# Gate and up projections by Strassen's seven products, SBUF as two arenas, branch and feed-forward tiles through HBM

## The chip, the core and the metric

The kernel runs on one core of a Trainium2 chip. The metric is the time of one execution on the device, in microseconds (us), from the first to the last instruction of the core. The engines are PE (TensorE: matmuls, with PEld for its weight loads), DVE (VectorE), ACT (ScalarE), POOL (GpSimd) and SP (SyncE, which here only issues loads). Each engine works through its own queue of instructions in order; a DMA is issued by one of these queues and ends later on its own.

## The reference, cut to what matters

One decoder block: 512 tokens, width 2048, two branches (latent attention, and a chunked spatial gate), a gated merge, an output projection, and a dense SwiGLU feed-forward of width 5632, all in float32.

```
a = rms_norm(h, g_mix);   z = a @ w_in                   # latents, u, v, gate logits
y_attn = mla(...) @ w_o_attn;   y_sgu = sgu(uv, ...) @ w_o_sgu
merged = sigmoid(g0) * y_attn + sigmoid(g1) * y_sgu
h = h + merged @ w_out
f = rms_norm(h, norm_ffn_g)
h = h + (silu(f @ w_gate_ffn) * (f @ w_up_ffn)) @ w_down_ffn   # [512,2048]x[2048,5632], twice
return rms_norm(h, norm_final_g)
```

## The kernel before

**Products in three passes.** Every float32 operand is split into a high part (an ACT cast to fp32r, line 94 for weights, 81 and 84 for other tiles) and a low part (a DVE subtraction, lines 95, 82, 85). A product is then three matmuls (`mm3`, lines 99 to 101): low by high, high by high, high by low.

**Weights.** `chunk` takes 512 KB of weights at a time: a load on the SP queue (line 93) into one of four `raw` buffers, the cast on ACT into one of three `whi`, the subtraction on DVE into one of three `wlo`. A load waits for the subtraction that read the buffer four chunks earlier. `gemm_fm` uses a chunk of 512 rows by 256 columns for 24 matmuls of 128x512 (feature-major: weights stationary, all 512 tokens moving); `gemm_tm` does the same token-major.

**Stages, in order.** Input statistics and latents, the shared rotary key, v and u of the spatial gate, its mixing (`L328`), transposes of the latents (`L341`), attention over eight pairs of heads, the attention branch, the gates and the merge, `w_out` with the residual, the feed-forward, the final norm. All tiles between the stages stay in SBUF, in one pool of 75 tiles of 512 columns.

**The feed-forward.** `norm_in` transposes the residual h between the four column blocks of `w_out` and splits it with the gain; the division by the root mean square is a factor per token and is put on the results instead (`rfb`, lines 582 and 584). `hidden(mp)` makes 256 columns of the hidden layer: gate and up together in four banks, 16 tiles of 128 rows deep, that is 2 x 16 x 2 x 3 = 192 matmuls of 128x512; 22 such steps make 4224. Then Silu (line 583), the product (585) and its split. After 8, 8, 8, 6, 6 and 8 rows of hidden tiles `down` uses them, so hidden and down alternate.

The engines' queues follow the order in which a scheduler puts the program's instructions; the rows of that order stand below where they matter.

Of the kernel before, what the change touches and what calls it, by code (L numbers as in the profile page):

```python
# [16 lines left out]
P = 128  # L17
# [7 lines left out]
G = 8  # L25
# [16 lines left out]
BIG, WR, WS = 75, 4, 3  # L42
FMAX = float(np.finfo(np.float32).max)


@with_exitstack
def tile_block(ctx: ExitStack, tc, a):
# [3 lines left out]
    big = ctx.enter_context(tc.tile_pool(name="big", bufs=BIG))  # L51
    wraw = ctx.enter_context(tc.tile_pool(name="wraw", bufs=WR))
    wsp = ctx.enter_context(tc.tile_pool(name="wsp", bufs=WS))
# [3 lines left out]
    def T(dt=F32):  # L57
        return big.tile([P, 512], dt, tag="t", name="t")
# [4 lines left out]
    def small(n, tag):  # L63
        return sml.tile([P, n], F32, tag="s%d" % n, name=tag)

# [8 lines left out]
    ones = con[:, C_ONE:C_ONE + P]  # L74

    def split(src, gain=None, n=512):
        hi, lo = T(F32R), T(F32R)
        if n < 512:
            hi, lo, src = hi[:, :n], lo[:, :n], src[:, :n]
        if gain is None:  # L80
            nc.scalar.copy(hi, src)  # L81
            nc.vector.tensor_tensor(out=lo, in0=src, in1=hi.bitcast(F32), op=ALU.subtract)  # L82
        else:
            nc.scalar.activation(hi, src, AF.Copy, scale=gain)
            nc.vector.scalar_tensor_tensor(
                out=lo, in0=src, scalar=gain, in1=hi.bitcast(F32), op0=ALU.mult, op1=ALU.subtract)
        return hi, lo

    def chunk(src, n=1024):
        raw = wraw.tile([P, 1024], F32, tag="raw", name="raw")  # L90
        hi = wsp.tile([P, 1024], F32R, tag="whi", name="whi")
        lo = wsp.tile([P, 1024], F32R, tag="wlo", name="wlo")
# [3 lines left out]
        return hi[:, :n], lo[:, :n]  # L96
# [6 lines left out]
    def gemm_fm(banks, w, kq, xs, first, last):  # L103
        """banks[m] += w[k-quad, 256 columns]^T @ xs (feature-major)."""
        hi, lo = chunk(w)
        hi = hi.rearrange("p (k m) -> p k m", k=4)
        lo = lo.rearrange("p (k m) -> p k m", k=4)
        for m, ps in enumerate(banks):
            ms = slice(m * P, (m + 1) * P)
            for k in range(4):  # L110
                xh, xl = xs[kq * 4 + k]
                mm3(ps, hi[:, k, ms], lo[:, k, ms], xh, xl, first and k == 0, last and k == 3)

    def gemm_tm(banks, w, kp, xs, first, last):
# [24 lines left out]
    def sumsq(parts, n, tag):  # L139
        """Sum of squares along the free axis of each list of tiles: [P, n]."""  # L140
        k = len(parts[0])
        acc = small(n * k, tag + "a")
        for i, tiles in enumerate(parts):
            for j, t in enumerate(tiles):
                junk = T()
# [7 lines left out]
    def row_bcast(r, tag):  # L153
        """[P, NB] per-token columns -> the same values along the free axis on each partition."""
        ps = PS()
        for tb in range(NB):
            dg = T()[:, :P]
            nc.vector.tensor_scalar(out=dg, in0=ident, scalar1=r[:, tb:tb + 1], scalar2=None, op0=ALU.mult)
            nc.tensor.matmul(ps[:, tb * P:(tb + 1) * P], ones, dg, start=True, stop=True)  # L159
        out = T()  # L160
# [4 lines left out]
    def load_x(xs, k):  # L165
        """Tiles 2k and 2k + 1 of the gained x, feature-major."""
        raw = wraw.tile([P, 1024], F32, tag="raw", name="raw")
        nc.sync.dma_start(raw, a["xT"][k])
        for j in range(2):
            v = V_MIX + k * 2 + j  # L170
            xs.append(split(raw[:, j * 512:(j + 1) * 512], vec[:, v:v + 1]))

# [3 lines left out]
    def x_stats(tb):  # L176
        for c in range(4):
            t, junk = T(), T()
            nc.sync.dma_start(t, a["x"][tb * P:(tb + 1) * P, c * 512:(c + 1) * 512])
            nc.scalar.activation(junk, t, AF.Square, accum_out=xacc[:, tb * 4 + c:tb * 4 + c + 1])  # L180

# [6 lines left out]
    lat = []  # L188
    lacc = cst.tile([P, 2 * NB], F32, name="lacc")
    def lat_out(g, banks):  # L190
        row = []
        for tb, ps in enumerate(banks):
            z, junk = T(), T()
# [22 lines left out]
    posi = big.tile([P, 512], I32, tag="t", name="posi")  # L216
# [11 lines left out]
    sinT = cst.tile([P, 512], F32, name="sinT")  # L228
    cosT = cst.tile([P, 512], F32, name="cosT")
# [3 lines left out]
    nc.scalar.activation(cosT, ang, AF.Sin)  # L233

    def rope(src):
        """The rotated [2 x 64 rope features, tokens]."""
        rot, out = T(), T()
# [4 lines left out]
        nc.vector.tensor_tensor(out=out, in0=out, in1=rot, op=ALU.add)  # L242
        return out

# [1 line left out]
    raw = wraw.tile([P, 1024], F32, tag="raw", name="raw")  # L246
    nc.sync.dma_start(raw, a["w_kpe"])
    kps = PS()
    for half in range(2):
        wk = wsp.tile([P, 1024], F32R, tag=("whi", "wlo")[half], name="wk").rearrange("p (k o m) -> p k o m", k=8, o=2)  # L250
# [7 lines left out]
    rxb = row_bcast(rx, "rxb")  # L258
    kpe = T()
    for own, other in ((slice(0, 64), slice(64, 128)), (slice(64, 128), slice(0, 64))):  # L260
        nc.scalar.copy(kpe[own], kps[other])
        nc.vector.tensor_tensor(out=kpe[own], in0=kps[own], in1=kpe[own], op=ALU.add)
    nc.vector.tensor_tensor(out=kpe, in0=kpe, in1=rxb, op=ALU.mult)
# [6 lines left out]
    vv = [[None, None] for _ in range(NB)]  # L270
    for g in range(2):
        banks = [PS() for _ in range(NB)]
        for kp in range(8):
            gemm_tm(banks, a["w_v"][g, kp], kp, aT, kp == 0, kp == 7)
        for tb, ps in enumerate(banks):
            t = T()
            nc.scalar.activation(t, ps, AF.Gelu_apprx_tanh, scale=rx[:, tb:tb + 1])
            vv[tb][g] = t
    rv = rsqrt(sumsq(vv, NB, "sv"), SGUW, NB, "rv")
    for tb in range(NB):  # L280
        for g in range(2):
            nc.vector.tensor_scalar(out=vv[tb][g], in0=vv[tb][g], scalar1=rv[:, tb:tb + 1], scalar2=None,
                                    op0=ALU.mult)

    kpe = rope(kpe)
    kph = cst.tile([P, 512], F32R, name="kph")
    kpl = cst.tile([P, 512], F32R, name="kpl")
    nc.scalar.copy(kph, kpe)
    nc.vector.tensor_tensor(out=kpl, in0=kpe, in1=kph.bitcast(F32), op=ALU.subtract)

    ut = []
    for mp in range(4):
        banks = [PS(), PS()]
        for kq in range(4):
            gemm_fm(banks, a["w_u"][mp, kq], kq, aT, kq == 0, kq == 3)
        for ps in banks:
            t = T()
            nc.vector.tensor_tensor(out=t, in0=ps, in1=rxb, op=ALU.mult)
            nc.scalar.activation(t, t, AF.Gelu_apprx_tanh)
            ut.append(t)  # L300

    wsT = []
    bsb = []
    for half in range(2):
        wt = wraw.tile([P, 1024], F32, tag="raw", name="raw")[:, :512]
        nc.gpsimd.dma_start(wt.rearrange("t (g s) -> t g s", g=4),
                            a["w_sgu"][half * 4:half * 4 + 4].rearrange("g t s -> t g s"))
        wm = wraw.tile([P, 1024], F32, tag="raw", name="raw")[:, :512]
        nc.gpsimd.affine_select(out=wm, in_=wt, pattern=[[0, 4], [-1, P]], compare_op=ALU.is_ge, fill=0.0,
                                base=0, channel_multiplier=1)  # L310
        ps = PS()
        for g in range(4):
            nc.tensor.transpose(out=ps[:, g * P:(g + 1) * P], in_=wm[:, g * P:(g + 1) * P], identity=ident)
        t = T()
        nc.vector.tensor_copy(t, ps)
        wsT.append(t)
        bt = T()
        nc.gpsimd.dma_start(bt, a["b_sgu"][half * 512:half * 512 + 512].partition_broadcast(P))
        bsb.append(bt)

# [1 line left out]
    latT = []  # L322
    for g in range(2):
        rows = []
        for k in range(4):
# [5 lines left out]
            rows.append(split(ps, vec[:, v:v + 1]))  # L331
        latT.append(rows)
    qnT, kvT = latT

# [1 line left out]
    sgT = []  # L336
    for g in range(G):
# [5 lines left out]
        t = T()  # L343
# [5 lines left out]
        nc.vector.tensor_tensor(out=t, in0=t, in1=ut[g], op=ALU.mult)  # L349
        sgT.append(t)  # L350
# [378 lines left out]
```

## Time and profile before

| | |
|---|---|
| time, median of 3 runs | 2789.36 us (2789.19 to 2790.16) |
| span of the profiled execution | 2788.1 us (the page gives no other time for it) |
| PE busy | 2769.5 us, 99% of the span |
| DVE, ACT busy | 1125.1 us (40%), 843.1 us (30%) |
| DMA | 280.07 MB, mean 100 GB/s |
| mean granted TensorE clock | 0.999 |

A row of a group names line, engine, operation, output<-inputs and shape, then how many there are, the busy time, the mean of one, and the idle time before them with what ended it. A row of the timeline has a start, a duration, the instruction, and in brackets the idle time before it with what ended that.

### The profile page before, as it was taken

Reading aid. Unit: us, or ns where it says so; the run is one execution under the profiler, and the core shown is the slowest. Engines: PE = TensorE matmul, PEld = TensorE weight load, DVE = VectorE, ACT = ScalarE, POOL = GpSimd, SP = SyncE. Lnnn points to the kernel's source line nnn. Section 1 sums busy time; section 2 is a strip of 40 time slices with the busy share of each in tenths; the row PEclk is TensorE's granted clock in tenths of the full one; section 3 lists DMA queues with packets and bytes.
Section 4 is the critical chain, followed back from the end, with each engine's and each line's share of the span. In section 5 each row is a group of like instructions: output and inputs, shape, how many; then the busy total and the mean of one; then the engine's idle time right before and its main releaser. Section 6 shows DMA issues by size and latency. Waiting matters only on the chain.

```text
span 2788.1 us, 30320 instructions
## 1 busy us (share of the span) xinstructions
PE 2769.5 (99%) x12712; PEld 2312.9 (83%) x12712; DVE 1125.1 (40%) x1470; ACT 843.1 (30%) x1195; POOL 15.4 (1%) x31
## 2 busy tenths in 40 slices
PE   8999999999999999999999999999999999999998
PEld 7888988888888888888888888888888888888887
DVE  3433867742433333532433333333333333343345
ACT  5332565621322222332322122212221222222223
POOL 0000000000000000100000000000000000000000
PEclk9999999999999999999999999999999999999999
DMA  7323211222423322432223323323222322223232
GB/s 249 101 91 96 79 53 54 70 90 97 154 97 98 98 98 93 153 102 91 91 98 98 99 92 98 98 98 99 94 96 98 98 99 96 94 98 98 99 121 91
DMA packets 79752, 280.07 MB, mean 100 GB/s; under 512 B 9152, under 2 KB 9152, under 8 KB 79616
## 3 DMA queue, kind: packets, MB, share of 16 engines
q1 hardware_dynamic: 76176, 268.99, 29.4%
q0 software_dynamic: 2000, 6.56, 0.7%
q10 hardware_dynamic: 1440, 2.60, 0.3%
q8 instruction: 99, 1.62, 0.2%
q14 instruction: 37, 0.30, 0.0%
HBM read 273.92 MB, written 4.19 MB: 100 GB/s over the span
## 4 chain that ended last, share of the span: by engine, by line
PE 99%; DVE 0%; DMA 0%; ACT 0%; issue 0%; SPq 0%
PE b L99 32%; PE b L101 32%; PE b L100 32%; PE b L446 1%; PE b L425 0%; PE b L426 0%; PE b L546 0%; PE b L341 0%; DMA raw<-in_w_lat 0%; PE b L328 0%; ACT whi L94 0%; DVE wlo L95 0%; PE b L159 0%; DVE t L266 0%; DVE t L82 0%
## 5 line engine op out<-in xcount | busy, mean ns | idle before, releaser
L95 DVE TENSOR_TENSOR wlo<-raw,whi 128x1024 fp32r<-128x1024 f32 (+1 forms) x480 | 583.3, 1216 | 1416.0 <-ACT whi L94 1415.7
L99 PE MATMUL b<-t,wlo 128*128 128x512 f32 x2592 | 1008.8, 389 | 0.0
L101 PE MATMUL b<-t,whi 128*128 128x512 f32 x2592 | 1008.5, 389 | 0.0
L100 PE MATMUL b<-t,whi 128*128 128x512 f32 x2592 | 1008.5, 389 | 0.0
L94 ACT CAST whi<-raw 128x1024 fp32r<-128x1024 f32 (+1 forms) x480 | 501.6, 1046 | 1588.7 <-PE b L101 977.2
L99 PEld LDWEIGHTS b<-t,wlo 128*128 128x128 f32 x2592 | 486.6, 188 | 101.5 <-DVE wlo L95 0.2
L101 PEld LDWEIGHTS b<-t,whi 128*128 128x128 f32 x2592 | 486.6, 188 | 100.9
L100 PEld LDWEIGHTS b<-t,whi 128*128 128x128 f32 x2592 | 486.6, 188 | 100.7
L99 PE MATMUL b<-whi,t 128*128 128x512 f32 (+1 forms) x1280 | 486.3, 380 | 7.9 <-ACT whi L94 7.9
L101 PE MATMUL b<-wlo,t 128*128 128x512 f32 (+1 forms) x1280 | 485.5, 379 | 0.0
L100 PE MATMUL b<-whi,t 128*128 128x512 f32 (+1 forms) x1280 | 485.3, 379 | 0.0
L99 PEld LDWEIGHTS b<-whi,t 128*128 128x128 f32 x1280 | 241.4, 189 | 52.7 <-ACT whi L94 7.9
L101 PEld LDWEIGHTS b<-wlo,t 128*128 128x128 f32 x1280 | 241.3, 188 | 45.8 <-DVE wlo L95 0.8
L100 PEld LDWEIGHTS b<-whi,t 128*128 128x128 f32 x1280 | 241.4, 189 | 45.1
L596 DVE TENSOR_TENSOR t<-b,t 128x512 f32<-128x512 f32 x96 | 66.1, 689 | 32.4 <-PE b L101 31.9
L81 ACT CAST t<-t 128x512 fp32r<-128x512 f32 x84 | 49.3, 623 | 98.4 <-DVE t L585 96.4
L82 DVE TENSOR_TENSOR t<-t 128x512 fp32r<-128x512 f32 x84 | 55.7, 689 | 32.9 <-ACT t L81 32.9
L99 PE MATMUL b<-t 128*128 128x512 f32 (+2 forms) x192 | 66.3, 346 | 1.2 <-DVE t L82 1.2
L100 PE MATMUL b<-t 128*128 128x512 f32 (+2 forms) x192 | 66.3, 345 | 0.0
L101 PE MATMUL b<-t 128*128 128x512 f32 (+2 forms) x192 | 66.2, 345 | 0.0
L82 DVE TENSOR_TENSOR t<-b,t 128x512 fp32r<-128x512 f32 (+1 forms) x96 | 58.2, 662 | 15.6 <-ACT t L81 15.3
L81 ACT CAST t<-b 128x512 fp32r<-128x512 f32 (+1 forms) x96 | 49.1, 586 | 30.0 <-PE b L101 29.8
(187 smaller groups left out, 950.3 us busy)
## 6 DMA issues: line engine op xcount, KB each, us to landing
raw<-in_w_gate SPq DMA_DIRECT2D x88, 512.0 KB, 3.3
raw<-in_w_up SPq DMA_DIRECT2D x88, 512.0 KB, 3.3
raw<-in_w_down SPq DMA_DIRECT2D x88, 512.0 KB, 3.3
raw<-in_w_g SPq DMA_DIRECT2D x64, 512.0 KB, 3.3
raw<-in_w_oattn SPq DMA_DIRECT2D x32, 512.0 KB, 3.3
raw<-in_w_out SPq DMA_DIRECT2D x32, 512.0 KB, 3.3
raw<-in_xT SPq DMA_DIRECT2D x16, 512.0 KB, 4.6
raw<-in_w_lat SPq DMA_DIRECT2D x16, 512.0 KB, 4.5
```

The lines of the kernel that those rows point to most:

```text
L81: nc.scalar.copy(hi, src)
L82: nc.vector.tensor_tensor(out=lo, in0=src, in1=hi.bitcast(F32), op=ALU.subtract)
L94: nc.scalar.copy(hi[:, :n], raw[:, :n])
L95: nc.vector.tensor_tensor(out=lo[:, :n], in0=raw[:, :n], in1=hi[:, :n].bitcast(F32), op=ALU.subtract)
L99: nc.tensor.matmul(ps, sl, mh, start=first, stop=False)
L100: nc.tensor.matmul(ps, sh, mh, start=False, stop=False)
L101: nc.tensor.matmul(ps, sh, ml, start=False, stop=last)
L446: nc.tensor.transpose(out=pb[b][:, c:c + P], in_=src, identity=ident)
L596: nc.vector.tensor_tensor(out=h[tb][c], in0=ps, in1=h[tb][c], op=ALU.add)
```

## The change

**Strassen.** Gate and up are each multiplied by a seven-product scheme. For 256 output columns, `pair_gemm` cuts the weights into quarters: even and odd tiles of 128 rows of depth, first and second 128 columns. The inputs are cut the same way: even and odd tiles, first and second 256 tokens. Seven products of 1024 rows deep, 128 columns by 256 tokens, replace eight: `product` has 8 x 3 = 24 matmuls of 128x256, a pair_gemm 168, and all 44 (22 gate, 22 up) 7392. The sums of weight quarters (s1 to s4) are four DVE instructions per pair_gemm, each of the seven forms is cast and subtracted as before (lines 701, 702), and the results are put together by one or two ACT copies (lines 736, 744) and DVE additions.

**Forms of the input.** The seven forms of the normalised input, high and low, are made once, before the feed-forward (`forms_x`). The norm is now a stage of its own: h is scaled by `rf`, transposed, gained, and each pair of tiles gives four sums, seven casts and seven subtractions of 256 columns.

**Arenas.** SBUF is two arenas, `ar` (fp32r, 144 units of 256 columns) and `af` (float32, 52 units), handed out by the program, least recently freed first. The forms take 112 units of `ar` in the feed-forward, which leaves 32 units, four pairs of a high and a low weight form. The raw weights of a pair_gemm take 16 units of `af` in one piece, filled by four loads of 512 KB.

**Tiles through HBM.** u, the mixed gate, attention outputs, the two branches' outputs, h and all hidden tiles are stored to HBM and loaded again where they are used, nearly all on the POOL queue. So hidden and down no longer alternate: all 44 pair_gemms first, then all of down. The rows of `w_o_sgu` come before the attention branch, the transposes of the latents earlier.

```diff
+    ar = Arena(cst.tile([P, NR * 256], F32R, name="ar"), NR)
+    af = Arena(cst.tile([P, NF * 256], F32, name="af"), NF, 32)
...
-    def hidden(mp):
-        nonlocal rfb
-        bg, bu = [PS(), PS()], [PS(), PS()]
...
+    def form_w(src):
+        hi, lo = ar.get(4), ar.get(4)
+        hv, lv = (t.rearrange("p (k m) -> p k m", m=P) for t in (hi, lo))
+        nc.scalar.copy(hv, src)
+        nc.vector.tensor_tensor(out=lv, in0=src, in1=hv.bitcast(F32), op=ALU.subtract)
+        return hi, lo
+
+    def product(ps, w, i, first):
+        hi, lo = w
+        for kp in range(8):
+            ks = slice(kp * P, (kp + 1) * P)
+            xh, xl = fx[kp][i][:, :256], fx[kp][i][:, 256:]
+            nc.tensor.matmul(ps, lo[:, ks], xh, start=first and kp == 0, stop=False, skip_group_check=True)
+            nc.tensor.matmul(ps, hi[:, ks], xh, start=False, stop=False, skip_group_check=True)
+            nc.tensor.matmul(ps, hi[:, ks], xl, start=False, stop=kp == 7, skip_group_check=True)
+        drop(w)
...
+    def pair_gemm(w):
+
+        raw = af.get(16)
         for kq in range(4):
-            gemm_fm(bg, a["w_gate"][mp, kq], kq, fT, kq == 0, kq == 3)
...
+            nc.sync.dma_start(raw[:, kq * 1024:(kq + 1) * 1024], w[kq])
+        quarters = raw.rearrange("p (k q m) -> p k q m", q=4, m=P)
+        a11, a21, a12, a22 = (quarters[:, :, q, :] for q in range(4))
+        ba, bb, bd = bank(), bank(), bank()
+        out = [T(), T()]
+        c11, c12, c21, c22 = out[0][:, :256], out[0][:, 256:], out[1][:, :256], out[1][:, 256:]
+        st = af.get(4)
+        s1 = st.rearrange("p (k m) -> p k m", m=P)
+        product(ba, form_w(a11), 0, True)
+        tt(s1, a21, a22, ALU.add)
+        s3 = tt(a21, a11, a21, ALU.subtract)
+        s2 = tt(a11, s1, a11, ALU.subtract)
+        uv = T()
+        u, u2 = uv[:, :256], uv[:, 256:]
+        nc.scalar.copy(u, ba)
+        product(bb, form_w(s2), 5, True)
+        tt(u2, bb, u, ALU.add)
+        product(bd, form_w(s3), 6, True)
+        product(bb, form_w(s1), 4, False)
+        tt(c22, bb, u, ALU.add)
+        tt(c22, bd, c22, ALU.add)
+        product(ba, form_w(a12), 1, False)
+        nc.scalar.copy(c11, ba)
+        s4 = tt(a12, a12, s2, ALU.subtract)
+        product(bb, form_w(s4), 2, False)
+        tt(c12, bb, u, ALU.add)
+        product(bd, form_w(a22), 3, False)
+        tt(c21, bd, u2, ALU.add)
+        drop(uv)
+        drop(raw, st)
+        return out
```

**Where instructions stand, inside a pair.** In the order's rows `af` and `ar` are the arenas, `b` a PSUM bank, `in_w_...` the weights in HBM. First the ACT queue before, in the middle of the feed-forward, where `hidden` passes into `down`:

```order
L94 CAST whi<-raw 128x1024 [waits DMAHW5_49,PE_49,Activation_49]
L583 ACTIVATE t<-t 128x512 [waits DVE_49]
L81 CAST t<-t 128x512 [waits DVE_49]
L94 CAST whi<-raw 128x1024 [waits DMAHW6_49,PE_49,Activation_49]
L94 CAST whi<-raw 128x1024 [waits DMAHW7_49,PE_49,Activation_49]
```

And the ACT queue now, from the two Silus of a gate to the end of the pair that follows (line 701: the high part of a form, in the order a11, s1, s3, a12, s2, s4, a22; line 736: the copy u of the first product; line 744: the copy c11):

```order
L701 CAST ar<-af 128x1024 [waits DMAHW2_49,DMAHW7_49,DMAHW1_49,DMAHW0_49]
L757 ACTIVATE af<-af 128x512 [waits DVE_49]
L701 CAST ar<-af 128x1024 [waits DVE_49,PE_49]
L701 CAST ar<-af 128x1024 [waits DVE_49]
L736 COPY af<-b 128x256 [waits PE_49]
L701 CAST ar<-af 128x1024 [waits Activation_49]
L701 CAST ar<-af 128x1024 [waits DVE_49]
L701 CAST ar<-af 128x1024 [waits DVE_49,PE_49,Activation_49]
L701 CAST ar<-af 128x1024 [waits PE_49]
L744 COPY af<-b 128x256 [waits PE_49]
```

The casts of weights, which waited before for a load and a free buffer alone, now have between the third and the fourth a copy that waits for PE's first product. On PE the order of the products is a11, the first ten matmuls of a12, s2, s3, s1, the rest of a12, s4, a22. The DVE queue now, across the border of two pairs (the first row is c21 of the old pair, the second the sum s1 of the new one, the third the product of gate and up; line 702 is the low part of a form, in the order a11, s1, s3, a12; the `128x8x128` rows between are s3 and s2):

```order
L107 TENSOR_TENSOR af<-b,af 128x256 [waits PE_49]
L107 TENSOR_TENSOR af<-af 128x1024 [waits DMAHW5_49,DMAHW6_49,DMAHW4_49,DMAHW3_49]
L107 TENSOR_TENSOR af<-af 128x512 [waits DVE_49]
L702 TENSOR_TENSOR ar<-af,ar 128x1024 [waits Activation_49]
L107 TENSOR_TENSOR af<-af 128x8x128 [waits DVE_49]
L702 TENSOR_TENSOR ar<-af,ar 128x1024 [waits Activation_49]
L107 TENSOR_TENSOR af<-af 128x8x128 [waits DVE_49]
L702 TENSOR_TENSOR ar<-af,ar 128x1024 [waits Activation_49]
L702 TENSOR_TENSOR ar<-af,ar 128x1024 [waits PE_49,Activation_49]
```

The low part of the new pair's first form stands behind c21, which waits for PE's last matmul of the old pair.

**Where instructions stand, the loads.** The SP queue before, in the same stage:

```order
L93 DMA raw<-in_w_gate 128x1024 [waits DMAHW5_49,DVE_49]
L93 DMA raw<-in_w_up 128x1024 [waits DMAHW6_49,DVE_49]
L93 DMA raw<-in_w_down 128x1024 [waits DMAHW7_49,DVE_49]
```

And now:

```order
L722 DMA af<-in_w_up 128x1024 [waits DMAHW3_49,DVE_49]
L722 DMA af<-in_w_up 128x1024 [waits DMAHW4_49]
L722 DMA af<-in_w_up 128x1024 [waits DMAHW5_49]
L722 DMA af<-in_w_up 128x1024 [waits DMAHW6_49]
L722 DMA af<-in_w_gate 128x1024 [waits DMAHW7_49,DVE_49]
```

Before, every load waited for DVE's subtraction on its own buffer; now the first of the four waits for DVE (the last low part taken from the one piece of raw weights, that of a22 of the pair before), and the other three go with it.

**Where instructions stand, at the start of the feed-forward.** The ACT queue before, after the last block of `w_out` (line 562 squares h, 84 splits a transposed tile, 94 casts the feed-forward's weights):

```order
L562 ACTIVATE t,facc<-t 128x512 [waits DVE_49]
L84 ACTIVATE t<-b,vec 128x512 [waits PE_49] x4
L129 ACT_TABLE_LOAD
L129 ACTIVATE rfr<-rfv 128x4 [waits DVE_49]
L94 CAST whi<-raw 128x1024 [waits DMAHW6_49,PE_49,Activation_49]
```

And now, at the end of the forms (line 691 gains a transposed tile, 669 casts a form of 256 columns, 701 is the first weight form):

```order
L691 ACTIVATE af<-b,vec 128x512 [waits PE_49]
L669 CAST ar<-af 128x256 [waits Activation_49] x2
L669 CAST ar<-af 128x256
L669 CAST ar<-af 128x256 [waits DVE_49] x4
L701 CAST ar<-af 128x1024 [waits DMAHW2_49,DMAHW7_49,DMAHW1_49,DMAHW0_49]
```

The casts of the first weights stood right behind the root mean square; now they stand behind all forms of the input.

## Rows read from the trace of the kernel before

**Rows 1.** The page's busy times, and the chain that ended last by engine.

```profile
PE 2769.5 (99%) x12712; PEld 2312.9 (83%) x12712; DVE 1125.1 (40%) x1470; ACT 843.1 (30%) x1195; POOL 15.4 (1%) x31
...
PE 99%; DVE 0%; DMA 0%; ACT 0%; issue 0%; SPq 0%
```

**Rows 2.** Timeline of PE: first and last of 26 matmuls of 512 columns.

```profile
1386.11 0.40 PE L100 MATMUL b<-t,whi 128*128 128x512 f32 x1
...
1391.78 0.39 PE L101 MATMUL b<-t,whi 128*128 128x512 f32 x1
```

**Rows 3.** Timeline of PE: first and last of 41 matmuls of 256 columns.

```profile
307.18 0.28 PE L101 MATMUL b<-wlo,t 128*128 128x256 f32 x1
...
311.97 0.28 PE L425 MATMUL b<-kph,t 128*128 128x256 f32 x1
```

**Rows 4.** DVE's groups by line and shape.

```profile
L95 DVE TENSOR_TENSOR wlo<-raw,whi 128x1024 fp32r<-128x1024 f32 x464 | 568.1, 1225 | 1396.7 <-ACT whi L94 1396.4
L82 DVE TENSOR_TENSOR t<-t 128x512 fp32r<-128x512 f32 x84 | 55.7, 689 | 32.9 <-ACT t L81 32.9
...
L95 DVE TENSOR_TENSOR wlo<-raw,whi 128x768 fp32r<-128x768 f32 x16 | 15.3, 955 | 19.3 <-ACT whi L94 19.3
...
L427 DVE CUSTOM_DVE_ANT_0 t<-b,con 128x256 f32<-128x256 f32 x16 | 6.8, 423 | 8.2 <-PE b L426 7.5
```

**Rows 5.** ACT's groups by line and shape.

```profile
L94 ACT CAST whi<-raw 128x1024 fp32r<-128x1024 f32 x464 | 488.9, 1054 | 1569.4 <-PE b L101 968.0 <-PE b L100 498.3 <-issue 98.4
...
L84 ACT ACTIVATE t<-b,vec 128x512 fp32r<-128x512 f32 x24 | 14.3, 684 | 0.0
L94 ACT CAST whi<-raw 128x768 fp32r<-128x768 f32 x16 | 13.4, 835 | 19.3 <-PE b L100 9.9 <-PE b L101 9.3
...
L434 ACT ACTIVATE t<-t,l 128x256 f32<-128x256 f32 x16 | 7.9, 494 | 0.0
...
L129 ACT ACT_TABLE_LOAD x4 | 5.1, 1283 | 0.1
...
L299 ACT ACTIVATE t<-t 128x512 f32<-128x512 f32 x8 | 5.0, 629 | 8.5 <-DVE t L298 8.5
```

**Rows 6.** Timeline of the tail: matmul, DVE, final scale.

```profile
2778.30 0.39 PE L101 MATMUL b<-t 128*128 128x512 f32 x1
2778.72 0.69 DVE L634 TENSOR_TENSOR t<-b,t 128x512 f32<-128x512 f32 x1 [0.55 <-PE b L101]
...
2781.78 1.33 ACT L647 ACTIVATE t<-t,ro3o 128x512 f32<-128x512 f32 x2 [1.00 <-DVE ro3o L136]
```

**Rows 7.** DMA issues: KB each, and median us from issue to landing.

```profile
raw<-in_w_gate SPq DMA_DIRECT2D x88, 512.0 KB, 3.3
...
raw<-in_w_uq SPq DMA_DIRECT2D x16, 384.0 KB, 3.1
...
out<-t SPq DMA_DIRECT2D x8, 256.0 KB, 2.9
...
raw<-in_w_sgu POOLq DMA_DIRECT2D x2, 256.0 KB, 4.2
t<-in_b_sgu POOLq DMA_DIRECT2D x2, 256.0 KB, 4.5
```

**Rows 8.** Windows: PE, PEld, DVE, ACT, POOL busy; then granted clock, DMA share, GB/s.

```profile
5.00:10.00 5.00, 2.04 (x4) 1.22 (x5) 3.50 (x5) 3.85 (x6) 0.00 (x0) 1.00 1.03 418
...
553.00:560.00 7.00, 5.78 (x41) 5.14 (x40) 6.72 (x10) 6.58 (x14) 0.00 (x0) 1.00 0.48 150
```

**Rows 9.** The chain in order of time: start, us, what.

```profile
1.25 5.55 DMA raw<-in_w_lat
...
281.74 3.49 PE b L328 x32
285.24 7.15 PE b L341 x64
...
1203.69 1.88 PE b L546 x16
```

**Rows 10.** Timeline of PE: the longest idle time inside the kernel.

```profile
557.60 0.50 PE L99 MATMUL b<-t 128*128 128x512 f32 x1 [1.22 <-DVE t L82]
```

**Rows 11.** Timeline of PE at the start: matmuls at the kernel's beginning.

```profile
9.78 0.63 PE L99 MATMUL b<-whi,t 128*128 128x512 f32 x1
...
13.19 0.53 PE L101 MATMUL b<-wlo,t 128*128 128x512 f32 x1
```

More of the change, by code (lines that the diff above doesn't have):

```diff
@@ L41, with __init__, get, put @@
 HALF_PI = float(np.float32(np.pi / 2))
-BIG, WR, WS = 75, 4, 3
+NR, NF = 144, 52
 FMAX = float(np.finfo(np.float32).max)
+class Arena:
+    def __init__(self, tile, units, keep=0):
+        self.tile, self.keep, self.clock = tile, keep, 0
+        self.free_at = [0] * units
+        self.held = {}
+    def get(self, n):
+        best = None
+        for i in range(0, len(self.free_at) - n + 1, n if n < 16 else 16):
+            span = self.free_at[i:i + n]
+            if None not in span:
+                cost = (n < 4 and i < self.keep, max(span), -i)
+                if best is None or cost < best[0]:
+                    best = cost, i
+        assert best, "arena is full"
+        i = best[1]
+        self.free_at[i:i + n] = [None] * n
+        ap = self.tile[:, i * 256:(i + n) * 256]
+        self.held[id(ap)] = ap, i, n
+        return ap
+    def put(self, *aps):
+        for ap in aps:
+            _, i, n = self.held.pop(id(ap))
+            self.clock += 1
+            self.free_at[i:i + n] = [self.clock] * n
 @with_exitstack
@@ L270, in tile_block, with latents @@
     vv = [[None, None] for _ in range(NB)]
[L271 to L319, printed above, removed]
     latT = []
-    for g in range(2):
+    def latents(g):
         rows = []
@@ new lines, in tile_block @@
+    qnT, kvT = latT
+    rv = rsqrt(sumsq(vv, NB, "sv"), SGUW, NB, "rv")
+    for tb in range(NB):
+        for g in range(2):
+            nc.vector.tensor_scalar(out=vv[tb][g], in0=vv[tb][g], scalar1=rv[:, tb:tb + 1], scalar2=None,
+                                    op0=ALU.mult)
+    rope(kp0, kpe)
+    kph = ar.get(2)
+    kpl = ar.get(2)
+    nc.scalar.copy(kph, kpe)
+    nc.vector.tensor_tensor(out=kpl, in0=kpe, in1=kph.bitcast(F32), op=ALU.subtract)
+    drop(kp0, kpe)
+    utd = drm.tile([G, P, 512], F32, name="utd")
@@ new lines, in tile_block @@
+    sgd = drm.tile([G, P, 512], F32, name="sgd")
+    for mp in range(4):
+        banks = [PS(), PS()]
+        for kq in range(4):
+            gemm_fm(banks, a["w_u"][mp, kq], kq, aT, kq == 0, kq == 3)
+        for i, ps in enumerate(banks):
+            t = T()
+            nc.vector.tensor_tensor(out=t, in0=ps, in1=rxb, op=ALU.mult)
+            nc.scalar.activation(t, t, AF.Gelu_apprx_tanh)
+            nc.scalar.dma_start(utd[mp * 2 + i], t)
+            drop(t)
+    drop(aT)
+    wsT = []
@@ L410, in scores @@
         pc = T()
-        out = []
+        out, tiles = [], [pc]
         for e in range(2):
             pa, pb = T(), T()
+            tiles += [pa, pb]
             dst = [pb[:, 384:512], pc[:, e * 256:e * 256 + 256], pb[:, 0:384], pa]
@@ L435, in scores @@
             out.append(dst)
-        return out
+        drop(qs, qp, ks)
+        return out, tiles
     def transposed(pr):
@@ new lines, in tile_block, with hidden @@
+    for mp in range(DFF // 256):
+        gate = pair_gemm(a["w_gate"][mp])
+        for t in gate:
+            nc.scalar.activation(t, t, AF.Silu)
+        for i, t in enumerate(pair_gemm(a["w_up"][mp])):
+            tt(t, t, gate[i], ALU.mult)
+            nc.gpsimd.dma_start(hidd[mp * 2 + i], t)
+            drop(t, gate[i])
+    drop(fx)
+    for tb in range(NB):
+        for c in range(4):
+            h[tb][c] = load(hd[tb, :, c * 512:(c + 1) * 512])
+    def hidden(k0, n):
+        return [move(load(hidd[k])) for k in range(k0, k0 + n)]
```

329 lines of the change are left out of this document (208 added, 121 removed).

## The prediction

> **What bounds the kernel now.** I read the page's busy times first, then the chain that ended last [rows 1]: PE is busy 99% of the span and the chain is PE for 99%, so before the change nothing but matmul issue counts. DVE is busy 40% and ACT 30%; what they do is hidden. What a matmul costs is read from starts in the timeline, not from the 0.39 us of a record, which overlaps its neighbours. 25 steps of 512 columns take 1391.78 - 1386.11 = 5.67 us, 0.2268 each [rows 2]; 40 steps of 256 columns, each with a weight load of its own, take 311.97 - 307.18 = 4.79 us, 0.1198 each [rows 3]. So halving the width costs 6% and not a whole load of weights. Two more views matter because the change takes work out from under PE's cover: the durations of DVE and ACT [rows 4, 5] and the landing times of loads [rows 7].
>
> **The change part by part.** The profiled execution has a span of 2788.1 us, 1.3 below the median of the runs; the sum is made on the span.
>
> Matmuls alone. Gate and up leave 4224 x 0.2268 = 958 us and bring 7392 x 0.1198 = 885.5 us: 72.5 us gained, if PE never waits. A pair_gemm is then 168 x 0.1198 = 20.1 us, a product 24 x 0.1198 = 2.88 us.
>
> Inside a pair PE does wait, and I walk through one by the queues, with 0 at the first matmul of product 1. A form costs 1.05 us on ACT and 1.23 on DVE [rows 4, 5]; a sum of two quarters has the same 1024 elements, so 1.23 too. DVE: s3 to 1.1, low of s1 to 2.3, s2 to 3.5, low of s3 to 4.8. ACT has cast s1 and s3 and stands at the copy u, which needs the end of product 1. The last matmul starts at 2.76, its result is free 0.42 us later [rows 6], so u starts at 3.2. No row has a 256-column copy from PSUM on ACT; 256 columns from SBUF take 0.49 with a scale, 512 from PSUM 0.68 with one [rows 5], and a fixed part with half of the rest gives 0.43; bounds 0.35 to 0.5. The cast of a12 stands behind it in ACT's queue: 3.65 to 4.7. Its low part on DVE: 4.8 to 6.0, and PE follows 0.1 later. So PE, done with product 1 at 2.9, goes on at 6.1: a stall of 3.2 us. It need not exist for the data (s3 and s1 have their forms early), but PE's order puts ten matmuls of a12 next. After that every form is ready before its product: the low part of s2 at 7.2, of s4 at 12.8, of a22 (its cast waits for the buffers of s3, free at 13.4) at 15.7, needed at 7.3, 17.7 and 20.6. PE ends at 3.2 + 20.1 = 23.3.
>
> At the border DVE has c21 ahead of everything of the new pair, and c21 needs the last matmul: start 23.6, 0.42 us (256 columns [rows 4]), then s1 1.23, low of a11 1.23, PE 0.1 later: 26.6. So a gate is followed by its up after 26.6 us. Between an up and the next gate the product of gate and up, 0.69 us [rows 4], stands between s1 and the low of a11: 27.3. Mean 27.0; 44 x 27.0 = 1188 us, **+230 us** against 958. Ends: 26.3 (copies and latencies at their low bounds) and 28.5 per pair, +199 and +296.
>
> The loads. Raw weights have in effect one place: the four loads of a pair wait for the low of a22 at 15.7. Beside one another they need the first landing, 3.3 us [rows 7], and 0.52 MB at 418 GB/s [rows 8], 1.25 us, for each of the other three: 7.1 us, landed at 22.8. With other traffic a 512 KB load took 5.55 us [rows 9], which makes 9.3 us, landed at 25.0. s1 can start at 24.0. So hidden by 1.2 us, or late by 1.0 us per pair, 44 us in all. I take hidden, and keep the other end.
>
> The start of the feed-forward. Before, the squares' root was hidden, and the first casts came right behind it. Now nothing of PE's can start until the forms are there. From the last matmul of w_out: DVE add, square, root and table load 4.8 us (the like chain of the tail, from matmul to final scale, takes 3.5 [rows 6], and the table load is 1.3 [rows 5]). Then DVE: 8 pairs of tiles x (4 sums + 7 subtractions) x 0.42 = 37 us, and 8 scales of 0.5 (an operation with two inputs of 512 columns takes 0.69 [rows 4], one with a single input less), 41 us; ACT: 56 casts of 0.43, 16 gains of 0.68, 8 scales of 0.7, 41 us also [rows 4, 5]. The last loads of the first weights need a slot that the last subtraction frees: 3.3 us, s1 and low of a11 2.5. Sum 51.9 us, less the transposes that PE did before in four groups of which [rows 9] shows one of 1.88, 7.5 us: **+44 us** (36 to 52; down if ACT and DVE overlap the loads better).
>
> From u to attention. The mixing used to follow at once, 3.49 and 7.15 us of PE with no gap [rows 9]. Now u passes through HBM and slots are reused in turn: u's last multiply and Gelu 1.3 us [rows 4, 5], store 2.9, mask 0.6 (an estimate by ACT's 0.63 for 512 columns [rows 5]), then a load of b_sgu 4.5, six DVE operations of 0.7, a store 2.9, the load of w_uq 3.1 and its parts 0.84 and 0.96 [rows 4, 5, 7], with latencies 22 us, in place of the 4.4 us of mixing that PE still does: **+18 us** (11 to 25). The store must not matter if its slot is not the next one given out, hence the low end.
>
> From the hidden tiles to down: 0.4 latency, four DVE operations 2.8, a slot, a load 3.3, a cast 1.05, with a little between: **+9 us** (5 to 12). The last pair of heads waits for tiles of the mixed gate: +1 (0 to 6). Attention, gates, w_out, down and tail keep their matmuls; their loads and stores lie under tens of microseconds of PE: 0 (-3 to +6).
>
> TensorE's clock. In the first 5.6 us matmuls start every 0.426 us (8 steps from 9.78 to 13.19 [rows 11]), the level of 1.2 GHz, with three before them; 12 matmuls at 0.426 in place of 0.227 cost 2.4 us. An idle time of 1.22 us [rows 10] left the granted clock of its window at 1.00 [rows 8]. I charge 2.4 for each of the three long gaps above, **+7 us**, and nothing for the gaps of 3.2 to 4.0 us inside pairs, though they are longer than the one seen to be harmless. The Trainium skill, page TensorE: Matmul & The Clock Gate, section HAM oscillation, says that waits between bursts of matmuls can put the engine back to half rate at every burst, so that the transition is paid each time; no trace before shows such a gap, and by that rule the second rival below would hold.
>
> Sum: 2788 + 230 + 44 + 18 + 9 + 1 + 7 = 3097 us span, about 3098 median. The gain of 72.5 us in matmuls is inside the 230.
>
> **The rivals.** A difference under 0.2%, 6 us, could not be told from no change.
> (a) The forecast, PE waiting twice in every pair: 3098, own range 3050 to 3180, chance 0.65.
> (b) Each stall also cools the clock: 88 x 2.4 = 211 us more, 3309. For it speaks the start [rows 11]; against it the 1.22 us gap [rows 10]. 0.12.
> (c) Loads late: one piece of raw weights. Four landings one after another, 4 x 3.3 = 13.2 us, would end at 28.9, 4.9 late, 3313; two at a time 2 us late, 88 us more, 3186. Each microsecond is 44. For it the 5.55 [rows 9], against it the 418 GB/s [rows 8]. 0.15, most of it near 3186.
> (d) The other side: PE runs on. If the copy u and c21 were served before PE needs what stands behind them, pairs would follow after 20.1 us, the 72.5 would be gained, and the other terms, 79 us here and 49 at their low ends, would leave 2795 down to 2765; it decides for faster where they come to under 72.5. The place is the two stalls in the walk above. Against it stands that both ACT and DVE serve their queues in order: every cast and subtraction of [rows 4, 5] that waited, waited at the head. 0.06, most of it below 2782.
> (e) Weight loads bind: each of the 7392 matmuls needs one, and at the mean of a load's record, 2312.9 / 12712 = 0.182 us [rows 1], the products alone would be 1345 us, 460 more than at 0.1198, so 3557 with the same stalls. [Rows 3] speak against it, where loads of that kind go by in 0.12. 0.02.
>
> **How the numbers follow.** The time is (a)'s, 3098. 3040 to 3250 holds (a) and most of (c); (b), (d) and (e), 0.20 together, are left out. Faster 0.05 and within 0.2% 0.01 are (d)'s; slower 0.94.
>
> **What would show it.** PE's busy share near 87%; in the feed-forward a period of some 27 us per 168 matmuls, with two idle times of 3 to 4 us, the first in front of L710 ended by DVE's low part (L702) and before that ACT's copy (L736), the second again by L702; one idle stretch of some 45 us in front of the first L710; matmuls of 256 columns at 0.12 us and a granted clock near 1.00. The prediction is wrong if the period is near 20 us, if DVE's s1 is seen waiting for DMA (then (c)), if starts inside pairs are 0.21 apart (then (b)), or if the start of the feed-forward is not idle.

## The result, and the profile after

The changed kernel takes 3215.05 us (median, 3207.11 to 3216.57), before 2789.28: a ratio of 1.152, interval 1.1504 to 1.1537. It is slower by 426 us; forecast were 309. The page's busy times, the granted clock in 40 slices, and the chain by engine, after:

```profile
PE 2878.7 (90%) x15872; PEld 2562.0 (80%) x15872; DVE 1526.3 (47%) x1985; ACT 1025.6 (32%) x1480; POOL 144.7 (5%) x271
...
PEclk9998999999999999978888988888898888999999
...
PE 72%; DVE 7%; DMA 6%; ACT 3%; issue 2%; SPq 1%; POOL 0%; DVEq 0%; POOLq 0%; ACTq 0%
```

Against [rows 1], PE has gone from 99% of the span to 90% and from 99% of the chain to 72%, although its matmuls have fewer columns in all. The row of the granted clock shows something that no row of before does: eights from the middle on. The windows of the stages, after: u to attention, the norm, the 44 pairs, and all behind them (the columns are those of [rows 8]; a pair is one `pair_gemm`):

```profile
284.64:312.68 28.04, 10.36 (x74) 9.66 (x73) 14.07 (x21) 2.74 (x4) 7.36 (x13) 0.74 0.56 183
1369.83:1416.94 47.11, 12.99 (x65) 11.21 (x65) 39.68 (x109) 36.77 (x88) 0.91 (x2) 0.64 0.31 103
1416.94:2709.80 1292.86, 1048.56 (x7392) 1029.86 (x7392) 680.95 (x744) 373.77 (x445) 34.63 (x65) 0.86 0.23 81
2722.28:3213.70 491.42, 482.00 (x2112) 398.20 (x2112) 206.74 (x272) 127.87 (x172) 17.45 (x33) 0.99 0.37 121
```

The pairs take 1292.9 us in place of 958, with two losses: PE is idle for 244 us, and its 7392 matmuls are busy for 1048.6 where 0.1198 each would make 885.5. The second loss is 163 us, and the granted clock of that window is 0.86.

One border and one pair, read off three engines. DVE after, where a gate ends and its up begins:

```profile
1487.33 0.42 DVE L107 TENSOR_TENSOR af<-b,af 128x256 f32<-128x256 f32 x1 [2.45 <-PE b L712]
1488.30 1.22 DVE L107 TENSOR_TENSOR af<-af 128x1024 f32<-128x1024 f32 x1 [0.54 <-DMA af<-in_w_up]
1489.44 1.22 DVE L702 TENSOR_TENSOR ar<-af,ar 128x1024 fp32r<-128x1024 f32 x1
...
1497.58 2.36 DVE L702 TENSOR_TENSOR ar<-af,ar 128x1024 fp32r<-128x1024 f32 x2 [2.38 <-ACT ar L701]
```

ACT after, behind product 1:

```profile
1496.23 0.37 ACT L736 COPY af<-b 128x256 f32<-128x256 f32 x1 [3.35 <-PE b L712]
1496.50 1.99 ACT L701 CAST ar<-af 128x1024 fp32r<-128x1024 f32 x2
```

PE after, the two gaps of that pair and the one that follows:

```profile
1490.71 0.58 PE L710 MATMUL b<-ar 128*128 128x256 f32 x1 [3.42 <-DVE ar L702]
1491.10 0.41 PE L711 MATMUL b<-ar 128*128 128x256 f32 x1
1491.31 0.41 PE L712 MATMUL b<-ar 128*128 128x256 f32 x1
...
1495.79 0.41 PE L712 MATMUL b<-ar 128*128 128x256 f32 x1
1498.86 0.39 PE L710 MATMUL b<-ar 128*128 128x256 f32 x1 [2.66 <-DVE ar L702]
...
1517.60 0.28 PE L712 MATMUL b<-ar 128*128 128x256 f32 x1
1521.27 0.58 PE L710 MATMUL b<-ar 128*128 128x256 f32 x1 [3.38 <-DVE ar L702]
```

The order of waits is the one walked through in the prediction. At the border c21 (1487.33) waits for PE, s1 (1488.30) stands behind it and here also waits 0.54 us for its load, the low of a11 (1489.44) behind s1, and PE starts at 1490.71. In the pair the copy u (1496.23) waits for product 1, the cast of a12 follows, its low part at 1497.58, and PE goes on at 1498.86. But the matmuls behind the gap start 0.21 us apart, 23 of them up to 1495.79, while those at 1517 stand 0.12 apart. The windows of the two stretches, with the granted clock as the third column from the right:

```profile
1490.71:1495.79 5.08, 5.08 (x24) 5.08 (x24) 4.49 (x4) 1.12 (x2) 0.00 (x0) 0.50 0.00 0
1503.00:1517.00 14.00, 14.00 (x119) 14.00 (x118) 4.84 (x7) 2.47 (x3) 0.44 (x1) 1.00 0.41 149
```

So the first stretch runs at the level of 1.2 GHz, as in [rows 11], after a gap of 3.42 us. Of the steps between neighbouring matmuls in the pairs some 1420 are longer than 0.17 us (gaps not counted; "slow steps" from here on); above 0.1198 each they make 132 us.

### The profile page after: what moved, and what is told of

The parts are those of the page before. It is cut to its first block, busy times and chain, and to the rows that moved or that the text cites. A ratio compares the mean times of both kernels' runs of the same rounds, so it can differ in the third digit from the quotient of the medians.

```text
span 3213.7 us, 38108 instructions
## 1 busy us (share of the span) xinstructions
PE 2878.7 (90%) x15872; PEld 2562.0 (80%) x15872; DVE 1526.3 (47%) x1985; ACT 1025.6 (32%) x1480; POOL 144.7 (5%) x271
## 4 chain that ended last, share of the span: by engine, by line
PE 72%; DVE 7%; DMA 6%; ACT 3%; issue 2%; SPq 1%; POOL 0%; DVEq 0%; POOLq 0%; ACTq 0%
PE b L150 15%; PE b L148 15%; PE b L149 15%; PE b L710 9%; PE b L712 8%; PE b L711 8%; DVE ar L702 4%; DVE af L107 2%; DMA af<-in_w_gate 2%; ACT ar L701 2%; DMA af<-in_w_up 2%; SPq L722 1%; PE b L522 1%; DMA af<-ogd 1%; ACT af L736 0%
## 5 line engine op out<-in xcount | busy, mean ns | idle before, releaser
L148 PE MATMUL b<-ar 128*128 128x512 f32 (+1 forms) x2656 | 1017.9, 383 | 40.9 <-ACT ar L142 20.3
L150 PE MATMUL b<-ar 128*128 128x512 f32 (+1 forms) x2656 | 1016.1, 383 | 0.2
L149 PE MATMUL b<-ar 128*128 128x512 f32 (+1 forms) x2656 | 1015.8, 382 | 0.0
L710 PE MATMUL b<-ar 128*128 128x256 f32 x2464 | 769.0, 315 | 260.7 <-DVE ar L702 260.7
L710 PEld LDWEIGHTS b<-ar 128*128 128x128 f32 x2464 | 538.4, 220 | 279.8 <-DVE ar L702 260.0
L711 PE MATMUL b<-ar 128*128 128x256 f32 x2464 | 758.1, 308 | 0.0
L712 PE MATMUL b<-ar 128*128 128x256 f32 x2464 | 756.3, 308 | 0.0
L143 DVE TENSOR_TENSOR ar<-af,ar 128x1024 fp32r<-128x1024 f32 (+1 forms) x304 | 365.2, 1209 | 606.2 <-ACT ar L142 544.6
L148 PEld LDWEIGHTS b<-ar 128*128 128x128 f32 x2656 | 502.2, 189 | 137.7 <-ACT ar L142 20.5
L150 PEld LDWEIGHTS b<-ar 128*128 128x128 f32 x2656 | 501.8, 189 | 98.0 <-DVE ar L143 1.5
L149 PEld LDWEIGHTS b<-ar 128*128 128x128 f32 x2656 | 502.4, 189 | 95.3
L142 ACT CAST ar<-af 128x1024 fp32r<-128x1024 f32 (+1 forms) x304 | 313.2, 1040 | 740.0 <-PE b L149 313.5
L711 PEld LDWEIGHTS b<-ar 128*128 128x128 f32 x2464 | 539.1, 219 | 0.0
L712 PEld LDWEIGHTS b<-ar 128*128 128x128 f32 x2464 | 538.0, 218 | 0.0
L701 ACT CAST ar<-af 128x1024 fp32r<-128x1024 f32 x308 | 318.3, 1047 | 593.0 <-PE b L712 347.3
L702 DVE TENSOR_TENSOR ar<-af,ar 128x1024 fp32r<-128x1024 f32 x308 | 372.5, 1221 | 178.0 <-ACT ar L701 177.9
L107 DVE TENSOR_TENSOR af<-af 128x1024 f32<-128x1024 f32 (+2 forms) x308 | 292.8, 963 | 30.1 <-ACT af L616 11.9
L107 DVE TENSOR_TENSOR af<-b,af 128x256 f32<-128x256 f32 x220 | 93.4, 424 | 416.4 <-PE b L712 414.7
L126 DVE TENSOR_TENSOR ar<-af,ar 128x512 fp32r<-128x512 f32 x100 | 66.5, 688 | 111.6 <-ACT ar L125 111.4
```

The costliest lines, as they stand in the source:

```text
L107: nc.vector.tensor_tensor(out=out, in0=in0, in1=in1, op=op)
L126: nc.vector.tensor_tensor(out=l, in0=src[:, :n], in1=h.bitcast(F32), op=ALU.subtract)
L148: nc.tensor.matmul(ps, sl, mh, start=first, stop=False)
L149: nc.tensor.matmul(ps, sh, mh, start=False, stop=False)
L150: nc.tensor.matmul(ps, sh, ml, start=False, stop=last)
L701: nc.scalar.copy(hv, src)
```

## The experiments

**Filling the gaps.** Is the slow spacing made by the gaps, or by the 256-column matmuls and the traffic? More matmuls, which write a bank that nobody reads, are put where PE would wait:

```diff
+        for j in range(fill):
+            ks = slice(j % 8 * P, (j % 8 + 1) * P)
+            nc.tensor.matmul(spare, hi[:, ks], fx[j % 8][i][:, :256], start=True, stop=True)
...
-        product(ba, form_w(a11), 0, True)
+        product(ba, form_w(a11), 0, True, 22)
...
-        product(bd, form_w(a22), 3, False)
+        product(bd, form_w(a22), 3, False, 24)
```

> The changed kernel with idle time filled: after product 1 of each pair 22 more matmuls of 128x256, after product 7 24 more, into a bank that nothing reads (the output is unchanged). PE's idle time in the pairs of the changed kernel is 258 us in 83 gaps, and 1420 of its 7392 matmuls start more than 0.17 us apart, 132 us in all above 0.12 each. Theory A (the idle gaps cool the clock): the added 2024 matmuls lie in the gaps, the matmuls of the pairs are back at 0.12 us, the granted clock is above 0.98, and the time falls by 100 to 135 us, to 3080 to 3115. Theory B (matmuls of 256 columns with a weight load each are slow by themselves, or the loads from HBM disturb them): the spacing stays, and the time is 3215 or more, up to 3400 if the added work comes on top.

Measured: 3067.18 us. 2024 matmuls more make the kernel 148 us faster. A window inside the pairs of this kernel:

```profile
1500.00:2200.00 700.00, 694.42 (x5768) 692.41 (x5767) 422.91 (x460) 228.49 (x269) 15.15 (x28) 1.00 0.25 93
```

The granted clock is back at 1.00 and 35 slow steps are left. Theory A holds, and B falls: the same matmuls with the same loads go at 0.12 us when nothing stands idle between them. The fall of 148 us is a little more than the 100 to 135 forecast.

**One gap at a time.** The same with only one of the two fills: the first kernel has the first of these lines, the second the second. The first was meant to leave only the border open, the second only the middle.

```diff
+        product(ba, form_w(a11), 0, True, 22)
...
+        product(bd, form_w(a22), 3, False, 24)
```

> Only the gap behind product 1 filled (22 matmuls per pair), the gap at the border of two pairs left at 2.8 to 3.4 us. With both filled, 1420 cold matmuls became 35 and the time fell from 3215 to 3067. Theory A (each gap cools the clock by itself, two per pair): about half of the cold matmuls stay, 3130 to 3150. Theory E (the clock falls only where two gaps lie close together, 9 us apart as here): with one of them filled it stays up, 3067 to 3085. Theory F (the border gaps alone do it, and the cold stretch merely reaches over the other gap): the spacing after the border stays, 3180 to 3215.

> Only the gap at the border filled (24 matmuls per pair), the one behind product 1 left at 2.7 us. Theory A: 3130 to 3150. Theory E: 3067 to 3085. Theory F: the clock stays up although a gap of 2.7 us is left in every pair, 3067 to 3085.

Measured: 3112.31 and 3113.50 us. The same window of both, in this order:

```profile
1500.00:2200.00 700.00, 620.88 (x4872) 610.95 (x4870) 395.78 (x433) 214.91 (x253) 14.10 (x26) 0.96 0.24 89
```

```profile
1500.00:2200.00 700.00, 636.76 (x4991) 630.88 (x4992) 404.27 (x442) 215.34 (x258) 14.10 (x26) 0.95 0.24 89
```

All three ranges missed, for both kernels. Only the second kernel is the test that it was meant to be. Its border is closed, its middle gap is left (42 gaps, 2.4 us in the mean), and some 590 slow steps remain. So the middle gap alone brings the clock down, and E and F fall.

The first kernel does not leave the border alone open. In its trace 14 or 15 of the 22 matmuls stand in front of product 1, at the border, and not behind it. The middle gap is still there, and the border is filled in part. PE's two longest waits in this kernel (line 715 is the fill; 15.9 us of the first row lie in front of the first pair):

```profile
PE b L710 <- DVE ar L702: 99.2, 41, 15.9
PE b L715 <- ACT ar L701: 49.4, 38, 5.0
```

Its slow steps, some 460, therefore belong to no single kind of gap. A kernel in which the border is the only long gap is the next one. Whether two gaps 9 us apart cost more than the same two gaps apart stays open, since the gaps have other lengths in each kernel.

**The place of one cast.** In this kernel the form of a12 is made in front of the copy u, so that ACT's cast need not wait for product 1:

```diff
+        f12 = form_w(a12)
         nc.scalar.copy(u, ba)
...
-        product(ba, form_w(a12), 1, False)
+        product(ba, f12, 1, False)
```

> The weight form of a12 is made ahead of the copy u in the program, nothing else. Theory A (in each pair PE waits because ACT's cast of a12 stands behind the copy u of product 1): the gap after product 1 shrinks from 2.7 us to 1 to 2 us, and with the shorter gaps some of the cold matmuls go: 3110 to 3180. Theory C (DVE's sums, not ACT's place in the queue, are late): the gap only moves to the next product, 3200 to 3230.

Measured: 3086.00 us, 129 faster, more than A's range. PE's waits in this kernel:

```profile
PE b L710 <- DVE ar L702: 174.0, 53, 16.4
...
PE b L710 <- ACT af L737: 20.6, 42, 1.6
```

The gap in the middle of a pair is now the wait for u itself (line 737 here), 0.49 us in the mean; the border's gaps are left, 3.7 us in the mean. 682 slow steps remain of 1420, so half of the gain is the stall (some 60 us of idle time) and half the clock (68 us): A's mechanism, with the clock priced too low again. The same window as above shows what the border's gaps do by themselves, a granted clock of 0.92:

```profile
1500.00:2200.00 700.00, 587.38 (x4432) 573.97 (x4432) 408.72 (x446) 221.33 (x263) 14.05 (x26) 0.92 0.25 90
```

**Where the raw weights lie.** The raw weights and the sums are given back to the arena in the other order. Since `af` hands out the place that has been free longest, consecutive pairs then alternate between two places:

```diff
-        drop(raw, st)
+        drop(st, raw)
```

> The raw weights and the sums of a pair are given back in the other order (drop(st, raw)), so that the raw weights of consecutive pairs alternate between two places and the next pair's loads start a pair earlier. Theory D (both stalls of a pair come from the single place of raw weights: its sums and casts cannot stand ahead of the old pair's last work in the queues): PE hardly waits between and in pairs, the period falls from 29.4 to about 21 us, the clock stays up, and the time is 2840 to 2900. Theory A (the stalls are made by the places of the copy u and of c21 alone, loads have little part): the late loads go (117 us of ACT's waiting are put down to them, of which some 20 to 40 reach PE), the stalls stay: 3150 to 3200.

Measured: 2862.78 us, ratio 1.0261 (1.0244 to 1.0278). Two words exchanged give back 352 of the 426 us. So D holds: the places in the queues that the prediction took as given are a result of the single place. The loads of the up that starts at 1490.71 in the changed kernel, and here those of a gate that starts at 1587.87:

```profile
1479.35 1.75 SPq L722 DMA_DIRECT2D af<-in_w_up  x4
```

```profile
1551.51 1.80 SPq L722 DMA_DIRECT2D af<-in_w_gate  x4
```

That is 11 us ahead of the pair in the changed kernel and 36 us here. With its weights there a pair earlier, the new pair's sums and forms are put ahead of the old pair's last work: the new pair's first matmul starts before c21 of the old one.

```profile
1587.87 0.28 PE L710 MATMUL b<-ar 128*128 128x256 f32 x1
1588.07 0.42 DVE L107 TENSOR_TENSOR af<-b,af 128x256 f32<-128x256 f32 x1
```

What is left are seven stalls of 4.7 us in 44 pairs, of this kind:

```profile
1568.19 0.58 PE L710 MATMUL b<-ar 128*128 128x256 f32 x1 [4.71 <-DVE ar L702]
```

**Both.** The two edits above in one kernel:

```diff
+        f12 = form_w(a12)
...
-        drop(raw, st)
+        drop(st, raw)
```

> Alternating places for the raw weights and the weight form of a12 ahead of the copy u, together. Seven stalls of 4.7 us are left with the alternating places alone (33 us), each in front of the product of a12. If they come from the cast of a12 behind the copy u, about two thirds of them go, with the cold matmuls behind them: 2835 to 2848 in place of 2863. If they come from DVE alone: 2855 to 2870.

Measured: 2829.88 us, 5 below the first range: the stalls are those of the cast behind u, and with them 108 of the 143 slow steps go. Of the 35 left, 13 stand at the first pair and 22 are the single step behind a gap. The gaps left inside the pairs take 0.46 to 1.35 us, and the granted clock between 1500 and 2200 us is 1.00 with them.

**Everything but Strassen.** Gate and up by `gemm_fm` on the 16 split tiles, all else as changed:

```diff
-            fx.append(forms_x(*pair))
+            fx.append(split(ps, vec[:, v:v + 1]))
...
+        for kq in range(4):
+            gemm_fm(banks, w[kq], kq, fx, kq == 0, kq == 3)
+        for t, ps in zip(out, banks):
+            nc.vector.tensor_copy(t, ps)
```

> Everything of the change but Strassen: arenas, tiles through HBM, all hidden tiles before down, the norm as a stage of its own; gate and up by the plain product with 128x512 matmuls, the normalised input split once into 16 tiles. This is the price of the rest: from u to attention 20 us, attention to w_out 12, the norm stage some 25 (16 splits in place of 56), the way to down 12, less the transposes: 2840 to 2870. If the stages around the feed-forward cost nothing by themselves, 2790; then all of the 426 us is Strassen's.

Measured: 2830.77 us, 41 above before and 9 below the range. The stages around, here with 16 splits in the norm in place of 56 forms, cost a tenth of the 426. PE's longest waits in this kernel:

```profile
PE b L148 <- DVE ar L143: 11.6, 1, 11.6
PE b L148 <- ACT ar L142: 7.9, 1, 7.9
PE b L148 <- ACT ar L125: 6.1, 1, 6.1
PE b L395 <- POOL af L391: 6.1, 1, 6.1
PE b L666 <- DVE af L662: 4.6, 1, 4.6
```

**Pairs in a pipeline.** Loads, sums and the first form of pair n + 1 are written in the middle of pair n; a12 is the second product, in a bank of its own:

```diff
+        f11 = form_w(a11)
...
+        yield
+        ba, be, bb, bd = bank(), bank(), bank(), bank()
...
+        product(ba, f11, 0, True)
+        product(be, form_w(a12), 1, True)
...
+        tt(c11, be, u, ALU.add)
...
+    def pair_gemm(n):
+        next(steps[n])
+        if n + 1 < len(steps):
+            next(steps[n + 1])
+        return next(steps[n])
```

> The pair_gemm of the changed kernel in program order with the next pair ahead: loads, sums and the form of a11 of pair n + 1 are written in front of the last two products of pair n, a12 is the second product in a bank of its own, the raw weights have two places and the sums two. All other stages are the changed kernel's. Theory D (PE waits in pairs only since nothing of the next pair can stand ahead of the old pair's last work): no stall over 1 us in the pairs, a granted clock near 1.00 there, a period near 20.3 us, and the time is that with alternating places less its 33 us of stalls and some 14 us of cold matmuls, 2810 to 2825. If DVE, which then has some 16 us of work per 20 us, becomes the bound: 2860 or more. It still is slower than before, by the stages around the feed-forward.

Measured: 2810.91 us, ratio 1.0078 (1.0061 to 1.0095). The window in the pairs:

```profile
1500.00:2200.00 700.00, 700.00 (x5785) 695.67 (x5785) 559.44 (x619) 280.01 (x309) 18.44 (x34) 1.00 0.32 118
```

5785 matmuls in 700 us are 0.1210 each and 20.3 us per pair, with PE never idle and DVE busy 80%. So Strassen does gain on PE what was counted, and it is the stages around that leave this kernel 22 us above before. Against the kernel without Strassen it is 20 us faster, of the 72.5. Where the other 52 went can be read from the windows of the norm, the pairs and the way to down in this kernel, and of the norm in the kernel without Strassen, whose PE goes from there to the end of down without a gap:

```profile
1369.98:1397.28 27.30, 13.61 (x65) 11.72 (x65) 26.41 (x75) 27.22 (x67) 0.00 (x0) 0.63 0.37 119
1397.28:2303.81 906.53, 900.05 (x7392) 893.85 (x7392) 724.40 (x817) 367.38 (x417) 35.64 (x67) 0.99 0.32 117
2303.81:2317.52 13.71, 0.00 (x2) 0.00 (x1) 7.58 (x13) 6.65 (x10) 5.29 (x10) 0.61 0.96 348
```

```profile
1370.88:1381.60 10.72, 9.93 (x61) 8.98 (x61) 9.02 (x17) 10.29 (x18) 0.00 (x0) 0.75 0.32 102
```

The norm takes 17 us more, the way to down 14, and the pairs 21 more than the 885.5 counted.

**The stages put back under PE.** On top of the pipeline: three quarters of the forms during w_out, unscaled, and the scale multiplied into the gate; the gate's mask ahead of u and its mixing in the first head pairs; earlier loads for the attention branch and for down:

```diff
+        if c < 2:
+            norm_in(c)
...
+                if kp == 4:
+                    norm_in(2)
...
+            tt(t, t, rfb, ALU.mult)
             nc.scalar.activation(t, t, AF.Silu)
+            nc.gpsimd.tensor_tensor(out=t, in0=t, in1=rfb, op=ALU.mult)
...
+            if pr < 2:
+                for g in range(4):
+                    mix(pr * 4 + g)
```

> The former, and the stages around it put back under PE: the forms of three quarters of the columns made during w_out (unscaled; the root mean square is multiplied into the gate's results, on DVE and POOL), the gate's mask and transposes ahead of u, its mixing spread over the first two head pairs, the attention outputs loaded during the rows of w_o_sgu, the first hidden tiles ahead of h. Each of these idle times has its own rows in the changed kernel: 20 us from u to attention, 44 in front of the feed-forward (about 20 of them left), 6 in front of the attention branch, 12 on the way to down. Theory (these terms add, since each is PE waiting on a chain): 2810 to 2825 less some 50 to 60 us, 2750 to 2770, faster than before by 1%. Rival (DVE and POOL, now with the work of two stages at a time, make PE wait elsewhere): 2790 to 2830.

Measured: 2758.38 us, ratio 0.9891 (0.9876 to 0.9906): faster than both kernels. The page's busy times, and the longest gaps left on PE behind the first load, in front of the feed-forward and on the way to down:

```profile
PE 2714.8 (99%) x15880; PEld 2413.6 (88%) x15880; DVE 1596.9 (58%) x2070; ACT 1012.2 (37%) x1428; POOL 217.0 (8%) x315
```

```profile
1366.30 0.58 PE L712 MATMUL b<-ar 128*128 128x256 f32 x1 [9.92 <-DVE ar L704]
...
2265.18 0.80 PE L148 MATMUL b<-ar 128*128 128x512 f32 x1 [4.99 <-ACT ar L142]
```

Together these edits give back 52 us, of 50 to 60 forecast, and the rival falls. What each of them gave was not run apart.

## Why the prediction was right, and where its size was off

The direction and the mechanism held: slower, because PE waits twice in every pair. The size was off by 117 us: 163 of busy time in the pairs above what was counted, most of it matmuls at the lower clock, less 58 because PE stood idle for a shorter time in the pairs than was counted, and 12 in the stages around. That 3215 lies between 3040 and 3250 is in part luck. It is above rival (a)'s own range, 3050 to 3180; the room above that had been left for late loads (c), which were small, and was filled by the clock (b), which the range left out.

**Matmuls alone.** 0.1198 us and 20.1 per pair: 0.1210 and 20.3 in the pipeline. Right; rival (e) falls.

**The two stalls.** Forecast 3.2 us in the middle and 3.3 or 4.0 at the border (26.6 or 27.3, less 23.3). From start to start, less 0.12, the rows above give 3.07 - 0.12 = 2.95 and 3.67 - 0.12 = 3.55 (the latter from an up to a gate). The copy u takes 0.37 in place of 0.43. PE is idle for 244 us in the pairs where 1188 - 885.5 = 302 were counted, since the gaps are shorter and some pairs have one gap in place of two. The walk was right, but it took the order as a given.

**TensorE's clock: the step that failed.** I charged 7 us for three long gaps and nothing for those inside pairs. They cost: 163 us of PE's busy time above the floor (132 of it in slow steps), and filling both gaps gives back 148. The gap of 1.22 us [rows 10] that did no harm was taken as evidence for gaps more than twice as long. Rival (b) had the mechanism, at 211 us, and its sign, starts 0.21 us apart inside pairs, is what the trace shows; the granted clock is 0.86 where near 1.00 was expected. The Trainium skill, page TensorE: Matmul & The Clock Gate, section HAM oscillation, says that waits between bursts of matmuls can bring half rate back at every burst; the trace agrees, with 0.86 granted over the pairs.

**Loads.** Forecast was that s1's operands land 1.2 us before it can start, or up to 1.0 late. What DVE's sums waited for in the pairs of the changed kernel (us, times):

```profile
  DMA af<-in_w_up: 7.3, 9
  DMA af<-in_w_gate: 3.1, 7
```

16 late loads and 10.4 us: hidden or nearly so, as forecast, and rival (c) in its own terms was small, though its sign, s1 waiting for DMA, was seen. The 6% of DMA in the chain are no measure of this price: where a load ends last by a few tenths of a microsecond, the chain runs through the whole load, and for most of that time PE was busy. But its cause, the single place, was the large one: not by when the loads land, but since the queues were filled as if nothing of the next pair could be had earlier.

**The other terms.** From u to attention +18 forecast; PE is idle for 17.7 of the 28.0 us of the window, and attention starts 20.3 later against [rows 9] (312.68 in place of 285.24 + 7.15). (In the kernel before, `L328` holds the transposes of the latents and `L341` the mixing, the other way round than the list of stages has it. The mixing still takes PE some 8 us after the change, where 4.4 were counted.) The norm 51.9 forecast (its parts add up to 51.6), 47.1 in its window; PE's idle time there, 34 us, is not one stretch of 45 but several, with transposes between and 16.4 as the longest. To down 9, and 12.5 between the third window and the fourth. Attention and the branches 1, but 11.5: w_out ends at 1369.83 against 1338.08, the start of the transposes behind it in this row of the chain before, of which 20.3 are u's.

```profile
1338.08 1.75 PE b L546 x16
```

Sum: 20.3 + 11.5 + (47.1 - 3.6 for the two groups of transposes that stood behind w_out before) + (1292.9 - 958) + 12.5 + 3 in down (482.0 busy, 2112 x 0.2268 = 479) = 426.

**Rival (d).** Its mechanism is what the pipeline makes: pairs without stalls. That gives 2811, not 2795, and with the other stages covered 2758. Its condition was right: for a gain the other terms have to come to less than 72.5 us.

## What to carry to other kernels

A stall on TensorE can be paid twice when it comes in every pass of a loop: once as idle time, once in the matmuls behind it at 1.2 GHz. Stalls of 2.4 to 3.7 us in the mean cost both here, those of 0.46 to 1.35 us in the kernel with both edits only the first. Count both, and read the granted clock over the window. Before a gap is put down to the order of a queue, ask why the order is so: here a buffer given back one place too early in a list of two kept the next pass's inputs from being ready, and exchanging two names was worth 352 us. Seven products in place of eight gained here only where the sums, casts and loads of the next pass already lay under the present one.

## What was not expected of the hardware

Adding 2024 useless matmuls made the kernel 148 us faster. Gaps of 2.7 to 3.4 us, twice per 30 us, brought the granted clock to 0.86 over 1.3 ms. The middle gap alone, 2.4 us in the mean, left 0.95 in the window above, and the border's alone, 3.7 us, 0.92. Not every such gap is followed by slow matmuls: in the kernel with the border filled, 27 slow steps stand behind the gap of 2.67 us that ends at 1500.25, and a single one behind that of 2.68 us that ends at 1555.11.
